# Squares queued behind splits, and a gates' and weight-sum workload spread over a recurrence, in a two-layer trunk kernel

## The chip, the cores and the metric

The kernel runs on one core of one Trainium2 chip. Five engines work at once, each through its own queue in order: TensorE (PE: matmuls), VectorE (DVE), ScalarE (ACT), GpSimd (POOL) and SyncE (SP, which here only issues transfers). ACT and POOL issue transfers too. The metric is the device time of one execution in microseconds; before the change the median of 3 runs is 1962.18 (1956.06 to 1965.04).

## What is computed

One sequence of 512 positions with 16 meta tokens ahead of it (T = 528), model width 2048, two residual layers and a final RMS norm, all in float32 at the interface:

```python
for layer in range(DEPTH):
    hn = rms_norm(h, norm_gain[layer])
    if layer % 2 == 0:
        y = even_mixer(...)   # GLU -> causal conv(31) -> LayerNorm -> swish, beside sparse attention; gates; @ w_out
    else:
        y = odd_mixer(...)    # 16 heads of a gated linear recurrence (HGRN2), RMS norm per head, gate; @ w_out
    h = h + y
h = rms_norm(h, final_norm_gain)
```

The sparse attention scores all keys with a small indexer, keeps the top 128 admissible ones of each query and attends to them with a shared relative bias. Most of the arithmetic lies in the dense projections: `hn @ w_in` and `@ w_out` of both layers.

## The kernel before

**Stripes.** A dense weight is cut into stripes of 128 output columns: 2048 x 128 float32, held as a [128, 2048] tile of 1 MB. A stripe goes through these steps: the load `w` (SP, L185, three buffers); a square with a running sum (ACT, L190, output `junk`); a sum over partitions, `tot` (POOL, L142); a power-of-two scale from it, `u`, `sc`, `inv` (DVE); the split of each half into a float16 high part `wh` (ACT, L206) and low part `wl` (DVE, L207), with five half buffers of each; then 96 matmuls into two banks of PSUM (48 into one bank for the stripes that need only 512 columns), three per block of 128 x 128: high by high, high by low, low by high (L245 to L247); and the evacuation (ACT or DVE). The names of weight tiles carry a number in the listings below: `w_476` and `w_669` are the first two split stripes of the even layer (the second is the first convolution stripe, g0), `w_791` and `w_947` the next two; `w_228` is an early stripe that is multiplied raw, without square and split. `w_8762` (before) and `w_8758` (after) are the first stripe of the even output projection.

**Stages.** The program loads x and its statistics, splits X0 (16 tiles `x`, L287 on ACT and L288 on DVE) and multiplies two stripes raw; then come the even layer's stripes with convolution (DVE, L576), indexer, softmax and attention between them; the even output projection of 16 stripes (S_OE), whose inputs MX are 16 split tiles, eight from the convolution branch (`x<-z`) and eight from the attention branch, which come back from DRAM (`mbd`) through the staging tile `mb`; the residual `h` (L764), also stored to `h1d`; the split X1; 16 heads of the recurrence, each with three stripes (fz, q, v) and some 70 small products (L833 to L972); 16 gates' stripes, whose scales are known by then (`gsc`); and the odd output projection, which works on pairs of stripes and on weight sums (`osum`, L1117).

**Early squares.** The scales of the gates' and the odd output projection's stripes come from squares taken ahead: `early_square` loads a whole stripe into a tile `gw` (one buffer, on ACT's queue, L745) and squares it. Those of the gates' stripes stand in the even output projection, one per stripe, the first gw load near the program's start; those of the odd output projection stand in the gates' stage, three per group for the first groups.

**Weight sums.** For seven pairs of odd output stripes, sums of half stripes are made in DRAM by transfers alone: 14 copies (SP, L324 and L325), 28 accumulating transfers (POOL, L327 and on) and 14 copies of one sum to the next (`os<-os`, SP, L330 and L334).

**What sets the order.** Each engine's queue is laid down when the program is built, by a planner that simulates it; of the work that could go next it takes that of the highest band: WGT (5), EVAC (4), SIDE (3), CONV (2). `tc.issue_after(ins)` puts what is issued under it behind that instruction in the same engine's queue; it adds no wait.

Of the kernel before, what the change touches and what calls it, by code (L numbers as in the profile page):

```python
# [74 lines left out]
def trunk_kernel(ctx: ExitStack, tc: tile.TileContext, x: bass.AP, w: bass.AP, wukv: bass.AP,  # L75
# [62 lines left out]

    EXP = float(2 ** 23)

    def all_sum(out, src, op=None):
        G.partition_all_reduce(out, src, channels=128, reduce_op=op or bass_isa.ReduceOp.add)  # L142
# [37 lines left out]
    def load_raw(s, pieces=1):  # L180

        w32 = wpool.tile([128, 2048], F32, name="w32", bufs=3)
        n = 2048 // pieces
        for i in range(pieces):
            Q.dma_start(w32[:, i * n:(i + 1) * n], w[s, :, i * n:(i + 1) * n])  # L185
# [16 lines left out]
    def split_weights(src, sc):  # L202

        hi = wpool.tile([128, 1024], F16, name="wh", bufs=5)
        lo = wpool.tile([128, 1024], F16, name="wl", bufs=5)
        S.activation(hi, src, AF.Identity, scale=sc)  # L206
        V.scalar_tensor_tensor(lo, src, sc, hi, op0=OP.mult, op1=OP.subtract)  # L207
        return hi, lo

    def load(s, back, keep=None, known=None):  # L210

        w32 = load_raw(s)
        if known is None:
            ss = wpool.tile([128, 1], F32, name="ss", bufs=4)
            square_sum(w32, ss)
            total = wpool.tile([128, 1], F32, name="tot", bufs=4) if keep is None else keep
            all_sum(total, ss)
            known = scales(total, back)
        sc, inv = known
        halves = [split_weights(w32[:, 1024 * n:1024 * (n + 1)], sc) for n in range(2)]  # L220
        return [h[0] for h in halves], [h[1] for h in halves], inv
# [98 lines left out]
    def sum_step(step, sa, sb, d):  # L320

        a1, a2, b1, b2 = w[sa, :, :1024], w[sa, :, 1024:], w[sb, :, :1024], w[sb, :, 1024:]
        if step == 0:
            Q.dma_start(d[0], b1)  # L324
            Q.dma_start(d[2], a1)  # L325
        elif step == 1:
            G.dma_start(d[0], b2, accum_op=OP.add)  # L327
            G.dma_start(d[2], b1, accum_op=OP.add)
        elif step == 2:
            Q.dma_start(d[1], d[0])  # L330
        elif step == 3:
            G.dma_start(d[1], a1, accum_op=OP.add)
        elif step == 4:
            Q.dma_start(d[3], d[1])  # L334
        elif step == 5:
            G.dma_start(d[3], a2, accum_op=OP.add)
# [369 lines left out]
    with band(SIDE):  # L706
        sums = cst([128, 8], F32, "mxb")
        for i in range(3):
            V.tensor_reduce(sums[:, i:i + 1], stat[:, i, :], axis=AX, op=OP.add)
        c = [sums[:, i:i + 1] for i in range(8)]  # L710
        sq = [vmax[:, i:i + 1] for i in range(6)]
        V.tensor_scalar(c[3], sq[2], 2048.0, None, op0=OP.mult)
        V.scalar_tensor_tensor(c[3], sq[3], 2.0, c[3], op0=OP.mult, op1=OP.add)
        V.tensor_tensor(c[3], c[3], c[0], op=OP.mult)
        V.scalar_tensor_tensor(c[4], c[2], 256.0, sq[4], op0=OP.mult, op1=OP.mult)
        V.tensor_tensor(c[4], c[4], c[1], op=OP.mult)
        V.tensor_tensor(c[3], c[3], c[4], op=OP.add)
# [20 lines left out]
    gss = r2p.tile([128, 16], F32, name="gss", bufs=1)  # L738
    gstat = r2p.tile([128, 16], F32, name="gstat", bufs=1)
    oss = r2p.tile([128, 16], F32, name="oss", bufs=1)  # L740

    def early_square(s, ss):
        with band(CONV):
            raw = wpool.tile([128, 2048], F32, name="gw", bufs=1)
            S.dma_start(raw, w[s])  # L745
            square_sum(raw, ss)
# [9 lines left out]
    for n in range(KT):  # L756
        with band(EVAC):
            while len(HIN) < min(KT, n + 3):
                residual0()
        hin = HIN[n]  # L760
        ps, inv = stripe(S_OE + n, MX, mback, order=(1, 0))
        with band(EVAC):
            for p, sl in ps:
                V.scalar_tensor_tensor(hin[:, sl], p, inv, hin[:, sl], op0=OP.mult, op1=OP.add)  # L764
# [12 lines left out]
    with band(EVAC):
        with tc.issue_after(last.ins):
# [62 lines left out]
    def rec_head(h, fz, q, v):  # L841
# [132 lines left out]
        V.tensor_tensor(on, o, rs, op=OP.mult)  # L974
        ON.append(on)

    for h in range(16):
        fz = ht([128, T], F32, "fz", 2)
        q = ht([128, SEQ], F32, "q", 2)
        v = ht([128, T], F32, "v", 2)  # L980
        if h == 0:
            with band(EVAC):
                evac(fz, ps0, rstd1)
        for dst, i in ((fz, 0), (q, 1), (v, 2)):
            if h or i:
# [25 lines left out]
        return t[:, :SEQ].bitcast(F16).rearrange("p (a b) -> p a b", a=2)  # L1011

    with band(SIDE):
        all_sum(gstat, gss)
# [12 lines left out]
        V.tensor_scalar(gs[:, 1:2], oscale, 0.5, None, op0=OP.mult)  # L1027

    def group(i):
# [3 lines left out]
        with band(SIDE):  # L1033
# [25 lines left out]
    with band(EVAC):  # L1059
        NP = KT // 2  # L1060
        opair = ht([128, NP], F32, "opair")
        V.tensor_reduce(opair, oss.rearrange("p (a b) -> p a b", b=2), axis=AX, op=OP.add)
        ototal = ht([128, NP], F32, "ototal")
        all_sum(ototal, opair)
        ou, osc, oinv = [ht([128, NP], I32, n) for n in ("ou", "osc", "oinv")]
        half_exponent(ou, ototal)
        V.tensor_scalar(osc, ou, -1.0, 204 * EXP, op0=OP.mult, op1=OP.add)
        V.tensor_scalar(oinv, ou, oback, None, op0=OP.add)
        osc, oinv = osc.bitcast(F32), oinv.bitcast(F32)
        oninv = ht([128, NP], F32, "oninv")  # L1070
        V.tensor_scalar(oninv, oinv, -1.0, None, op0=OP.mult)
# [227 lines left out]
```

## Time and profile before

| | us |
|---|---|
| median of 3 runs | 1962.18 |
| profiled execution | 1966.32 |
| its span | 1964.5 |
| PE busy | 1837.5 (94%) |
| DVE busy | 1340.1 (68%) |
| ACT busy | 1202.3 (61%) |
| POOL busy | 184.3 (9%) |

The profile is of one execution. A row of a timeline gives start, length, engine, line, operation, and in brackets the engine's idle time ahead of it with what ended it. A row of waits gives engine, name and line that waited, then what it waited for, with the total, the count and the longest. A wait is put down to the releaser that came last. The granted clock of PE is 1.00 at full speed and 0.50 at half.

### The profile page before, as it was taken

How to read it: one execution, taken by the hardware profiler on the slowest of the kernel's cores; microseconds unless marked ns; L12 is line 12 of the kernel's file. 1: busy time of each engine (PE TensorE's matmuls, PEld its weight loads, DVE VectorE, ACT ScalarE, POOL GpSimd, SP SyncE). 2: the span in 40 equal slices, each digit the busy share in tenths (PEclk: the TensorE clock that was granted, in tenths of full speed). 3: DMA queues.
4: the chain of work that ended last, by engine and by line, in shares of the span. 5: the costliest groups of instructions: out<-in, count | busy, mean ns of one | idle time of the engine just before them, and what ended most of it. 6: DMA issues, size and time to landing. Idle time of an engine off the chain costs nothing.

```text
span 1964.5 us, 36557 instructions
## 1 busy us (share of the span) xinstructions
PE 1837.5 (94%) x14934; PEld 1410.8 (72%) x14934; DVE 1340.1 (68%) x2752; ACT 1202.3 (61%) x1881; POOL 184.3 (9%) x324
## 2 busy tenths in 40 slices
PE   8499999888999989698989999999999999999997
PEld 6367668776888778487767777777777775445886
DVE  7249999997737335443468777787778776666775
ACT  5366566434555565675467776777677787545563
POOL 2122111001121210100010000000000000001000
PEclk9699999998999999799999999999999999999998
DMA  9997233222334324765422222222222266225653
GB/s 314 294 283 209 86 103 107 96 71 90 110 115 120 123 61 128 255 246 194 152 97 87 70 83 87 87 84 71 84 87 87 96 227 236 106 89 203 214 194 108
DMA packets 60825, 272.78 MB, mean 139 GB/s; under 512 B 7760, under 2 KB 15224, under 8 KB 39440
## 3 DMA queue, kind: packets, MB, share of 16 engines
q1 hardware_dynamic: 38592, 195.04, 27.6%
q0 software_dynamic: 15152, 37.51, 8.6%
q10 hardware_dynamic: 6912, 37.88, 5.3%
q8 instruction: 117, 1.92, 0.4%
q14 instruction: 52, 0.43, 0.1%
HBM read 251.30 MB, written 40.58 MB: 149 GB/s over the span
## 4 chain that ended last, share of the span: by engine, by line
PE 42%; issue 5%; DMA 5%; ACT 3%; DVE 1%; POOL 0%; ACTq 0%; DVEq 0%; POOLq 0%
PE mps L245 10%; PE mps L246 10%; PE mps L247 10%; PE mps L1117 8%; DMA gw<-in_w_dram 3%; DMA w<-in_w_dram 2%; ACT junk L190 2%; PE s L837 1%; PE s L838 1%; PE s L839 1%; PE po L960 1%; PE po L959 1%; PE s L956 0%; ACT wh L206 0%; DVE wl L207 0%
## 5 line engine op out<-in xcount | busy, mean ns | idle before, releaser
L245 PE MATMUL mps<-x,wh 128*128 128x264 f16 (+1 forms) x3440 | 1023.8, 298 | 70.6 <-ACT x L287 30.7
L246 PE MATMUL mps<-x,wh 128*128 128x264 f16 (+1 forms) x3440 | 1023.9, 298 | 4.2 <-DVE x L288 4.0
L247 PE MATMUL mps<-x,wl 128*128 128x264 f16 (+1 forms) x3440 | 1022.7, 298 | 0.4 <-DVE wl L207 0.4
L245 PEld LDWEIGHTS <-wh 128*128 128x128 f16 x3456 | 341.0, 99 | 167.1 <-issue 35.8
L246 PEld LDWEIGHTS <-wh 128*128 128x128 f16 x3456 | 341.1, 99 | 149.3 <-issue 37.4
L247 PEld LDWEIGHTS <-wl 128*128 128x128 f16 x3456 | 340.9, 99 | 121.2 <-issue 8.7
L207 DVE SCALAR_TENSOR_TENSOR wl<-w,sc,wh 128x1024 f16<-128x1024 f32 x224 | 287.1, 1285 | 141.3 <-ACT wh L206 133.1
L206 ACT ACTIVATE wh<-w,sc 128x1024 f16<-128x1024 f32 x224 | 254.4, 1144 | 152.8 <-PE mps L246 141.7
L190 ACT ACTIVATE junk<-w 128x2048 bf16<-128x2048 f32 (+1 forms) x116 | 216.2, 1864 | 144.6 <-DMA w<-in_w_dram 132.8
L576 DVE SCALAR_TENSOR_TENSOR z<-u,vec,z 128x528 f32<-128x528 f32 x240 | 179.3, 764 | 1.3
L142 POOL PARTITION_ALL_REDUCE tot<-ss x96 | 47.0, 489 | 885.9 <-ACT junk L190 885.9
L146 DVE TENSOR_SCALAR u<-tot 128x1 int32<-128x1 int32 x96 | 14.5, 151 | 152.0 <-POOL tot L142 151.8
L1117 PEld LDWEIGHTS <-wh 128*128 128x128 f16 x912 | 89.2, 98 | 11.0 <-issue 0.3
L206 ACT ACTIVATE wh<-w,osc 128x1024 f16<-128x1024 f32 x53 | 60.8, 1151 | 56.6 <-PE mps L1117 46.1
L207 DVE SCALAR_TENSOR_TENSOR wl<-w,osc,wh 128x1024 f16<-128x1024 f32 x53 | 67.8, 1283 | 30.5 <-ACT wh L206 30.4
L190 ACT ACTIVATE junk<-gw 128x2048 bf16<-128x2048 f32 x32 | 61.1, 1911 | 35.6 <-DMA gw<-in_w_dram 35.4
L1117 PE MATMUL mps<-on,wh 128*128 128x256 f16 x464 | 78.2, 273 | 0.1
L207 DVE SCALAR_TENSOR_TENSOR wl<-w,gsc,wh 128x1024 f16<-128x1024 f32 x32 | 41.1, 1283 | 37.4 <-ACT wh L206 37.2
L833 ACT ACTIVATE qhm<-q 128x256 f16<-128x256 f32 x128 | 51.7, 415 | 19.7 <-DVE q L935 14.6
L1117 PE MATMUL mps<-on,wl 128*128 128x256 f16 x232 | 63.2, 273 | 0.0
L834 DVE SCALAR_TENSOR_TENSOR qlm<-q,qhm 128x256 f16<-128x256 f32 x128 | 52.6, 421 | 11.1 <-ACT qhm L833 9.1
L206 ACT ACTIVATE wh<-w,gsc 128x1024 f16<-128x1024 f32 x32 | 36.6, 1145 | 23.3 <-PE mps L246 23.3
(430 smaller groups left out, 2756.1 us busy)
## 6 DMA issues: line engine op xcount, KB each, us to landing
w<-in_w_dram SPq DMA_DIRECT2D x132, 1024.0 KB, 4.9
gw<-in_w_dram ACTq DMA_DIRECT2D x32, 1024.0 KB, 4.9
os<-in_w_dram POOLq DMA_DIRECT2D x28, 512.0 KB, 18.3
w<-os SPq DMA_DIRECT2D x28, 512.0 KB, 4.2
w<-in_w_dram SPq DMA_DIRECT2D x23, 512.0 KB, 4.2
os<-in_w_dram SPq DMA_DIRECT2D x14, 512.0 KB, 21.4
os<-os SPq DMA_DIRECT2D x14, 512.0 KB, 12.3
h<-in_x_dram POOLq DMA_DIRECT2D x16, 264.0 KB, 5.2
```

Source lines behind the costliest of these rows:

```text
L142: G.partition_all_reduce(out, src, channels=128, reduce_op=op or bass_isa.ReduceOp.add)
L190: S.activation(junk[:, :src.shape[-1]], src, AF.Square, accum_out=ss)
L206: S.activation(hi, src, AF.Identity, scale=sc)
L207: V.scalar_tensor_tensor(lo, src, sc, hi, op0=OP.mult, op1=OP.subtract)
L245: P.matmul(o, hi[half][:, ws], xh[:, sl], start=n == 0 and k == 0, stop=False)
L246: P.matmul(o, hi[half][:, ws], xl[:, sl], start=False, stop=False)
L247: P.matmul(o, lo[half][:, ws], xh[:, sl], start=False, stop=n == 1 and k == 7)
L576: eng.scalar_tensor_tensor(z, u[:, j:j + T], col(V_CW + i * CW + j), z, op0=OP.mult, op1=OP.add)
L833: S.activation(hi, src, AF.Copy, scale=scale)
L834: V.scalar_tensor_tensor(lo, src, scale, hi, op0=OP.mult, op1=OP.subtract)
L837: P.matmul(out, kh, qh, start=True, stop=False)
L1117: P.matmul(p, wt[:, sl], xt, start=start and k == i == 0, stop=stop and k == 7 and i == 2, skip_group_check=stop and not start and resume)
```

## The change

Five things, by the diff:

1. In `load` a stripe's square is put, by `behind("S")`, behind the last split that was issued so far on ACT.
2. The gates' early squares leave the even output projection. They come in the recurrence: per head, two loads of half a stripe (two buffers) and, a head later, two squares of 1024 columns; `gsum` adds the halves.
3. The weight sums leave the start. `waves` lays out 56 transfers, `send` issues 1, 2 and 1 of them behind the `all_sum` of the three stripes of each head, all from POOL.
4. The eight attention tiles come back from DRAM through the staging names Kh, Vt and L (three buffers each), and seven of their splits go to new tiles `mx` of their own.
5. The odd output projection's early squares become halves too, one stripe per gates' stripe, behind a split, and their scales come in two blocks (`pair_scales`).

```diff
+    queued = {}
+
     def all_sum(out, src, op=None):
-        G.partition_all_reduce(out, src, channels=128, reduce_op=op or bass_isa.ReduceOp.add)
+        queued["G"] = G.partition_all_reduce(out, src, channels=128, reduce_op=op or bass_isa.ReduceOp.add)
...
-        S.activation(hi, src, AF.Identity, scale=sc)
+        queued["S"] = S.activation(hi, src, AF.Identity, scale=sc)
...
+    def behind(name):
+        return tc.issue_after(queued[name].ins) if name in queued else ExitStack()
...
-            square_sum(w32, ss)
+            with behind("S"):
+                square_sum(w32, ss)
...
+    def sum_steps(sa, sb, d):
 
         a1, a2, b1, b2 = w[sa, :, :1024], w[sa, :, 1024:], w[sb, :, :1024], w[sb, :, 1024:]
...
+        return [[(d[0], b1, 0), (d[2], a1, 0)], [(d[0], b2, 1), (d[2], b1, 1)], [(d[1], d[0], 0)],
+                [(d[1], a1, 1)], [(d[3], d[1], 0)], [(d[3], a2, 1)]]
+
+    def waves(first, sums):
+
+        steps = [sum_steps(first + 2 * p, first + 2 * p + 1, d) for p, d in enumerate(sums)]
+        return [t for h in range(len(sums) + 5) for p in range(len(sums)) if 0 <= h - p < 6 for t in steps[p][h - p]]
+
+    def send(todo, n):
+        with band(CONV), behind("G"):
+            for _ in range(min(n, len(todo))):
+                dst, src, add = todo.pop(0)
+                G.dma_start(dst, src, accum_op=OP.add if add else OP.bypass)
...
-            mb = et([128, T], F32, "mb", 2)
+            shape, name = (([128, T], "Kh"), ([128, 5, 128], "Vt"), ([128, T], "L"))[i // 3]
+            mb = et(shape, F32, name, 3)
...
-            MX[8 + i] = split(r1p.tile([128, 2, T], F16, name="x", bufs=KT), mb, c[7])
+            MX[8 + i] = split(r1p.tile([128, 2, T], F16, name="mx" if i < 7 else "x", bufs=7 if i < 7 else KT), mb, c[7])
...
+    def early_load(s):
+        for o in (0, 1024):
+            raw = ht([128, 1024], F32, "gw", 2)
+            S.dma_start(raw, w[s, :, o:o + 1024])
+            raws.append(raw)
...
-        early_square(S_G + n, gss[:, n:n + 1])
...
+    todo = waves(S_OO, osum)
...
+                send(todo, 1 + i % 2)
...
-            for p in range(7):
-                sum_step(h - p, S_OO + 2 * p, S_OO + 2 * p + 1, osum[p])
+            if h:
+                for c in range(2):
+                    square_sum(raws.pop(0), gss[:, h - 1, c:c + 1])
+            early_load(S_G + h)
...
+            with band(CONV), behind("S"):
+                if raws:
+                    for c in range(2):
+                        square_sum(raws.pop(0), oss[:, ahead - 1, c:c + 1])
+                if ahead < KT:
+                    early_load(S_OO + ahead)
+                ahead += 1
+            if ahead in (9, 17):
+                pair_scales(ahead // 16)
-        for n in range(3 * i, min(3 * i + 3, KT)):
-            early_square(S_OO + n, oss[:, n:n + 1])
         group(i)
```

What stands in the queues. On ACT, from the statistics to the first splits (L190 and L192 are the square, L206 and L208 the split of a weight, L287 and L293 that of X0), before and then after:

```order
L190 ACTIVATE junk,ss<-w_476 128x2048
L305 ACTIVATE rstd<-po,eps_r 128x264
L305 ACTIVATE rstd<-s_288,eps_r 128x264
L306 ACTIVATE rstd<-rstd 128x264 x2
L206 ACTIVATE wh<-w_476,sc 128x1024 x2
L287 ACTIVATE x<-sq,gains 128x528 x13
L190 ACTIVATE junk,ss<-w_669 128x2048
L287 ACTIVATE x<-sq,gains 128x528 x3
L437 ACTIVATE sq<-gb 128x528
L206 ACTIVATE wh<-w_669,sc 128x1024 x2
```

```order
L192 ACTIVATE junk,ss<-w_669 128x2048
L293 ACTIVATE x<-sq,gains 128x528 x3
L208 ACTIVATE wh<-w_669,sc 128x1024 x2
L192 ACTIVATE junk,ss<-w_791 128x2048
L293 ACTIVATE x<-sq,gains 128x528
L420 ACTIVATE kih<-gt 128x528
L293 ACTIVATE x<-sq,gains 128x528 x2
L208 ACTIVATE wh<-w_791,sc 128x1024
L293 ACTIVATE x<-sq,gains 128x528 x4
L459 ACTIVATE z<-s_607 8x352
L293 ACTIVATE x<-sq,gains 128x528 x2
L208 ACTIVATE wh<-w_791,sc 128x1024
```

The square of `w_669` now stands ahead of all X0 splits and its split behind three of them, and the square of `w_791` ahead of the other thirteen. In SP's queue the load of `w_669` stands right behind that of `w_476`; before, the 14 copies of the weight sums stood between them.

On ACT, at the end of the even layer's stripes and the first stripes of the output projection (`gw` are gates' stripes, `x<-z` the splits of the convolution branch), before and then after:

```order
L287 ACTIVATE x<-z,mxb 128x528 x8
L190 ACTIVATE junk,gss<-gw 128x2048
L767 ACTIVATE acc_8621<-h_8625 128x528
L772 DMA h1d<-h_8625 128x528
L190 ACTIVATE junk,ss<-w_8762 128x2048
L745 DMA gw<-in_w_dram 128x2048
L190 ACTIVATE junk,gss<-gw 128x2048
L190 ACTIVATE junk,ss<-w_8893 128x2048
L745 DMA gw<-in_w_dram 128x2048
L206 ACTIVATE wh<-w_8762,sc 128x1024 x2
L206 ACTIVATE wh<-w_8893,sc 128x1024 x2
```

```order
L208 ACTIVATE wh<-w_8758,sc 128x1024
L274 ACTIVATE gt<-mps,inv 128x264
L591 ACTIVATE gb<-gt 128x528
L293 ACTIVATE x<-L,mxb 128x528
L293 ACTIVATE x<-z,mxb 128x528 x6
L208 ACTIVATE wh<-w_8758,sc 128x1024
L192 ACTIVATE junk,ss<-w_8885 128x2048
L293 ACTIVATE x<-z,mxb 128x528
L274 ACTIVATE gt<-mps,inv 128x264
L703 ACTIVATE gt<-z 128x528
L274 ACTIVATE gt<-mps,inv 128x264
L591 ACTIVATE gb<-gt 128x528
```

The split of the first output stripe now stands among the MX splits, with no gates' square ahead of it; before, three squares and two loads stood between the last MX split and it.

On POOL, in the first heads of the recurrence, after the change (`tot` is the sum of a stripe's squares, `os` a weight sum in DRAM):

```order
L144 ISA tot<-ss 128x1
L341 DMA os_156<-os_155 16x8192
L878 MEMSET vt 128x128
L144 ISA tot<-ss 128x1
L341 DMA os_159<-in_w_dram 128x1024
L144 ISA tot<-ss 128x1
L341 DMA os_161<-in_w_dram 128x1024
L341 DMA os_163<-in_w_dram 128x1024
L144 ISA tot<-ss 128x1
L341 DMA os_165<-in_w_dram 128x1024
```

Before, this queue held in this stage only `tot` and the clearing of `vt`; each transfer now stands behind one stripe's `tot` and ahead of the next one's.

More of the change, by code (lines that the diff above doesn't have):

```diff
@@ L184, in load_raw @@
         for i in range(pieces):
-            Q.dma_start(w32[:, i * n:(i + 1) * n], w[s, :, i * n:(i + 1) * n])
+            queued["Q"] = Q.dma_start(w32[:, i * n:(i + 1) * n], w[s, :, i * n:(i + 1) * n])
         return w32
@@ L318, in trunk_kernel @@
     osum = [[dram.tile([128, 1024], F32, name=f"os{p}{i}") for i in range(4)] for p in range(7)]
-    def sum_step(step, sa, sb, d):
+    def sum_steps(sa, sb, d):
         a1, a2, b1, b2 = w[sa, :, :1024], w[sa, :, 1024:], w[sb, :, :1024], w[sb, :, 1024:]
[L323 to L336, printed above, removed]
+        return [[(d[0], b1, 0), (d[2], a1, 0)], [(d[0], b2, 1), (d[2], b1, 1)], [(d[1], d[0], 0)],
[8 more added lines that the diff above has]
+                G.dma_start(dst, src, accum_op=OP.add if add else OP.bypass)
     r1 = tc.tile_pool(name="r1", bufs=KT, side="left")
@@ L722, in trunk_kernel @@
         for i in range(8):
-            mb = et([128, T], F32, "mb", 2)
+            shape, name = (([128, T], "Kh"), ([128, 5, 128], "Vt"), ([128, T], "L"))[i // 3]
+            mb = et(shape, F32, name, 3)
+            if len(shape) > 2:
+                mb = mb.rearrange("p a b -> p (a b)")[:, :T]
             Q.dma_start(mb, mbd[i])
-            MX[8 + i] = split(r1p.tile([128, 2, T], F16, name="x", bufs=KT), mb, c[7])
+            MX[8 + i] = split(r1p.tile([128, 2, T], F16, name="mx" if i < 7 else "x", bufs=7 if i < 7 else KT), mb, c[7])
         for i in range(8):
@@ L737, in trunk_kernel @@
     back1 = xscale[1][1]
-    gss = r2p.tile([128, 16], F32, name="gss", bufs=1)
+    gss = r2p.tile([128, 16, 2], F32, name="gss", bufs=1)
     gstat = r2p.tile([128, 16], F32, name="gstat", bufs=1)
[L740 to L746, printed above, removed]
+    oss = r2p.tile([128, 16, 2], F32, name="oss", bufs=1)
+    raws = []
+    def early_load(s):
[3 more added lines that the diff above has]
+            raws.append(raw)
     H1 = []
@@ L766, in trunk_kernel @@
             if n == 0:
-                S.activation(acc1, hin, AF.Square)
+                done = S.activation(acc1, hin, AF.Square)
             else:
                 sq = U.tile([128, T], F32, name="sq1", bufs=3)
-                last = S.activation(sq, hin, AF.Square)
+                done = S.activation(sq, hin, AF.Square)
                 V.tensor_tensor(acc1, acc1, sq, op=OP.add)
             S.dma_start(h1d[n], hin)
-        early_square(S_G + n, gss[:, n:n + 1])
     with band(WGT):
@@ L777, in trunk_kernel @@
     with band(EVAC):
-        with tc.issue_after(last.ins):
+        with tc.issue_after(done.ins):
             S.preload_act_table_set("natural_log_exp_and_others")
@@ L1013, in trunk_kernel @@
     with band(SIDE):
-        all_sum(gstat, gss)
+        for c in range(2):
+            square_sum(raws.pop(0), gss[:, 15, c:c + 1])
+        gsum = ht([128, 16], F32, "gsum")
+        V.tensor_reduce(gsum, gss, axis=AX, op=OP.add)
+        all_sum(gstat, gsum)
         gu = ht([128, 16], I32, "gu")
@@ L1041, in group, with pair_scales @@
             FB[i] = split(form_slot(SLOTS[2 * i + 1]), xb, gs[:, 1:2])
+    oq = ht([128, 5, 8], F32, "oq")
+    osc, oinv, oninv = oq[:, 2, :].bitcast(I32), oq[:, 3, :].bitcast(I32), oq[:, 4, :]
+    def pair_scales(c):
+        sl = slice(4 * c, 4 * c + 4)
+        with band(EVAC):
+            V.tensor_reduce(oq[:, 0, sl], oss[:, 8 * c:8 * c + 8, :].rearrange("p (a b) c -> p a (b c)", b=2),
+                            axis=AX, op=OP.add)
+            all_sum(oq[:, 1, sl], oq[:, 0, sl])
+            u = ht([128, 4], I32, "ou", 2)
+            half_exponent(u, oq[:, 1, sl])
+            V.tensor_scalar(osc[:, sl], u, -1.0, 204 * EXP, op0=OP.mult, op1=OP.add)
+            V.tensor_scalar(oinv[:, sl], u, oback, None, op0=OP.add)
+            V.tensor_scalar(oninv[:, sl], oinv[:, sl].bitcast(F32), -1.0, None, op0=OP.mult)
+    ahead = 1
+    early_load(S_OO)
     for i in range(8):
@@ L1054, in trunk_kernel @@
                 V.scalar_tensor_tensor(ON[h], ON[h], col(V_RG + h), g[:, :SEQ], op0=OP.mult, op1=OP.mult)
-        for n in range(3 * i, min(3 * i + 3, KT)):
-            early_square(S_OO + n, oss[:, n:n + 1])
-        group(i)
[L1059 to L1071, printed above, removed]
+            with band(CONV), behind("S"):
+                if raws:
+                    for c in range(2):
+                        square_sum(raws.pop(0), oss[:, ahead - 1, c:c + 1])
[4 more added lines that the diff above has]
+                pair_scales(ahead // 16)
+        group(i)
+    osc, oinv = osc.bitcast(F32), oinv.bitcast(F32)
     acc2 = ht([128, SEQ], F32, "sg", 2)
```

## The prediction

> **What bounds the kernel now.** I read the table of stretches first, then what TensorE (PE) waits for, then the timelines around each wait. TensorE is busy almost all of the span, so only stretches in which it is not, or runs at a lower granted clock, have time to give.
>
> Stretches (start:end, length, then busy time and instructions of PE, weight load, DVE, ACT, POOL, then granted clock, DMA share, GB/s):
>
> ```profile
> 40.00:80.00 40.00, 14.21 (x103) 12.03 (x102) 12.76 (x21) 6.24 (x8) 8.70 (x13) 0.71 1.03 271
> 80.00:120.00 40.00, 38.41 (x255) 26.21 (x255) 14.15 (x27) 23.13 (x31) 7.23 (x13) 0.87 1.00 293
> 200.00:360.00 160.00, 159.81 (x1152) 117.19 (x1151) 155.31 (x334) 95.64 (x164) 19.48 (x28) 1.00 0.32 105
> 360.00:490.00 130.00, 109.77 (x878) 90.86 (x877) 113.58 (x242) 52.90 (x86) 14.63 (x25) 0.95 0.26 80
> 780.00:830.00 50.00, 31.87 (x246) 25.19 (x245) 23.14 (x38) 31.28 (x38) 9.13 (x18) 0.80 0.65 232
> 1030.00:1600.00 570.00, 569.00 (x5433) 442.48 (x5431) 441.00 (x1042) 422.18 (x712) 19.38 (x58) 1.00 0.25 91
> 1600.00:1640.00 40.00, 37.84 (x298) 24.59 (x297) 27.34 (x60) 32.28 (x53) 0.00 (x0) 1.00 0.61 225
> ```
>
> PE loses 26 of 40 us at 40–80, 20 of 130 at 360–490, 18 of 50 at 780–830, and 1 of 570 in the recurrence, which is PE-bound. The waits of PE (us in total, times, longest) name who comes last:
>
> ```profile
> PE mps L245 <- ACT x L287: 30.7, 7, 27.2
> PE mps L245 <- ACT wh L206: 15.3, 1, 15.3
> ...
> PE mps L245 <- DVE h L764: 9.8, 6, 2.7
> ...
> PE s L538 <- DMA uh<-ql: 5.4, 2, 3.8
> ```
>
> Most of it is ACT. In the list for all engines, ACT itself waits mostly in front of squares (L190), for their loads:
>
> ```profile
> ACT junk L190 <- DMA w<-in_w_dram: 132.8, 46, 28.5
> ACT junk L190 <- DMA gw<-in_w_dram: 35.4, 22, 5.8
> ```
>
> A queue runs in order, so a square that waits for its load holds up the splits and evacuations behind it. That is what the parts of the change touch.
>
> **1. The start (T1).** ACT's timeline; the bracket is idle time before the row and its releaser:
>
> ```profile
> 32.42 1.98 ACT L287 ACTIVATE x<-sq,gains 128x528 f16<-128x528 f32 x3
> 37.68 1.99 ACT L287 ACTIVATE x<-sq,gains 128x528 f16<-128x528 f32 x3 [3.29 <-DVE sq L383]
> ...
> 49.49 0.74 ACT L287 ACTIVATE x<-sq,gains 128x528 f16<-128x528 f32 x1 [1.24 <-DVE sq L383]
> 78.70 1.91 ACT L190 ACTIVATE junk<-w 128x2048 bf16<-128x2048 f32 x1 [28.48 <-DMA w<-in_w_dram]
> ...
> 99.82 0.48 ACT L563 ACTIVATE gt<-mps,inv 128x264 f32<-128x264 f32 x1 [2.22 <-PE mps L247]
> ```
>
> Thirteen of the sixteen X0 splits are done at 50.2; the other three stand behind the square of w_669, whose load lands only at 78.7. The last evacuation of that stripe, g0, is at 99.82. SP's queue and the page's list of DMA issues (KB, median us to landing) say why the load is late:
>
> ```profile
> 43.90 7.97 SPq L185 DMA_DIRECT2D w<-in_w_dram  x3
> ```
> ```profile
> w<-in_w_dram SPq DMA_DIRECT2D x132, 1024.0 KB, 4.9
> ...
> os<-in_w_dram SPq DMA_DIRECT2D x14, 512.0 KB, 21.4
> ```
>
> w_669 is issued at 43.90, behind the 14 os copies, into DMA engines that are full (share 1.03) with them, the POOL accumulates and a gw load. In the change nothing of this is ahead of w_669, which goes out right behind w_476 and should be there when its square comes up near 30. Next late: the square of w_791. It stands behind the first three X0 splits and the split of w_669, ahead of the other thirteen, and its buffer is that of the raw stripe w_228, still being multiplied. SP got all three buffers by 43.9 + 8.0 = 51.9, so that load lands between 43.9 + 4.9 = 48.8 and 56.8. I take 49: square done at 51. Then thirteen splits at the pace shown (ten from 37.68 to 50.23, 1.25 each) are 16.3, the two splits of w_791 2.2, and I allow 3.5 for evacuations between: the last X0 at 73. The order leaves about 69 matmuls of g0 behind it. One matmul, in the out-projection where they run close:
>
> ```profile
> 888.75 0.27 PE L245 MATMUL mps<-x,wh 128*128 128x264 f16 x1 [1.71 <-DVE h L764]
> 888.87 0.27 PE L246 MATMUL mps<-x,wh 128*128 128x264 f16 x1
> ```
>
> 0.113 from start to start, so 7.8: g0 ends near 81 against 99.8. **T1 = −18**; with the load at 56.8 and something over for a slow clock it is −8, with no blocking at all −27, the whole wait.
>
> **2. The attention's first scores (T2).**
>
> ```profile
> 147.24 0.39 PE L538 MATMUL s<-kih,uh 128*128 128x256 f32 x1 [3.83 <-DMA uh<-ql]
> ```
>
> The 5.4 of waits there (list above) are a small transfer behind the same full DMA engines. In the stretch that follows, and in one of part 4, the granted clock is 0.50 (the columns as in the first table):
>
> ```profile
> 804.10:821.20 17.10, 3.64 (x17) 2.23 (x18) 5.73 (x10) 11.12 (x13) 0.76 (x2) 0.50 0.55 198
> 148.70:155.50 6.80, 6.10 (x26) 4.66 (x27) 5.68 (x10) 3.23 (x6) 0.00 (x0) 0.50 1.04 266
> ```
>
> PE is busy 6.1 of 6.8 us at half speed, so up to 3 more is lost. The transfers are gone from there; I take 5.4 and half of that 3: **T2 = −7** (0, if the copy itself is slow, to −8).
>
> A clock of one half after a long wait is also a rule of the Trainium skill ("TensorE: Matmul & The Clock Gate", Part 1): the clock halves after an idle window of about 3.4 us and comes back after a busy one. The trace agrees: its half-clock stretches above last 6.8 and 17.1 us, two and five such windows. By the rule alone each removed long wait would also give half of one such window; the sum uses the stretches of the trace.
>
> **3. Even stripes at 374–482 (T3).** The waits of PE in that stretch alone:
>
> ```profile
> PE mps L245 <- ACT gt L268: 7.3, 6, 2.6
> ...
> PE mps L245 <- ACT gt L563: 5.6, 5, 1.5
> ```
>
> These 12.9 are on a bank of PSUM whose evacuation, by the order, stands behind another item in ACT's queue. The new order puts one square between two splits at a fixed place, and fewer stripes start both banks on the one just before. But DVE is busy 113.6 of 130 there, so the stretch may not shrink much: **T3 = −6** (0 to −13), half of the waits.
>
> **4. Into the even out-projection (T4).** ACT again, then PE:
>
> ```profile
> 798.58 1.90 ACT L190 ACTIVATE junk<-gw 128x2048 bf16<-128x2048 f32 x1
> ...
> 810.91 1.91 ACT L190 ACTIVATE junk<-gw 128x2048 bf16<-128x2048 f32 x1 [5.79 <-DMA gw<-in_w_dram]
> ...
> 814.91 4.26 ACT L206 ACTIVATE wh<-w,sc 128x1024 f16<-128x1024 f32 x4
> ```
> ```profile
> 817.14 0.40 PE L245 MATMUL mps<-x,wh 128*128 128x264 f16 x1 [15.30 <-ACT wh L206]
> ```
>
> The splits of the first two out-projection stripes stand behind two squares of gates' stripes (gw) and a 5.79 wait for one; PE stands 15.3. In the change no gw is there, and w_8758's square and split stand among the MX splits. What goes: 15.3, some 2 of the smaller X waits ahead of it (the rest of the 30.7 above beside 27.2 is 3.5), and half of the 3.6 that PE ran at half clock (row 804.10). **T4 = −19** (−8, if the mx splits from DRAM hold ACT up, to −21.6).
>
> **5. Out-projection stripes (T5).** The chain of waits repeats itself each 12.7 us (start, length, what):
>
> ```profile
> 901.07 6.18 DMA w<-in_w_dram
> ...
> 909.37 2.01 ACT junk L190 x2
> 911.37 1.05 ACT wh L206
> 912.44 1.29 DVE wl L207
> 913.75 6.12 DMA w<-in_w_dram
> ```
>
> One load, two squares (one for the stripe, one for the gates), split, and the next load into the buffer that this frees: 6.2 + 2.0 + 2.0 + 1.1 + 1.3 = 12.6. A split waits for the square of a later stripe, and that one for a load that needs the split's buffer. With the square behind the split the loop is broken; PE's own 96 × 0.113 = 10.8 is left. Five or six stripes: 9.8 of waits and one lower-clock window. **T5 = −11** (−5 to −11.3).
>
> **6. The recurrence (T6, T7).** Its last head and the gates' start lose 2.2 of 40 (row 1600); gw squares then go behind no load: **T6 = −2** (0 to −2). Added to each of 16 heads: two squares of 1024 (2 × 1.0), two DMA issues, four transfers from POOL. The nearest rows for ACT that full and for POOL's issues:
>
> ```profile
> 1560.00:1612.00 52.00, 51.37 (x455) 36.58 (x453) 33.54 (x73) 43.62 (x68) 0.59 (x2) 1.00 0.56 204
> ```
> ```profile
> 27.95 0.93 POOL L327 DMA_DIRECT2D os<-in_w_dram  x1 [21.15 <-DMA os<-in_w_dram]
> ```
>
> With ACT at 84% and DMA at 0.56 PE loses 0.63 in 52; over 590 us that is 7. The added work gives ACT 74 + 6 = 80%. **T7 = +6** (0 to +32, two a head, as in the last one).
>
> The moved MX staging, gsum, the halved odd squares and pair_scales lie beside PE-bound stretches (160–360, 1640–1945) and cost nothing while ACT has a quarter free; without that cover some 2 us.
>
> Sum: −18 − 7 − 6 − 19 − 11 − 2 + 6 = −57. The profiled execution is 1966.3, 4.1 above the median of the runs, so 1909 there, **1905** as a median.
>
> **Rivals.**
> A. The even stage is bound by DVE (155 of 160 us busy at 200–360, 113.6 of 130 after). Then an earlier start only makes DVE's backlog wait later: T1 to T3 (31) come back, 1936. Against it: DVE had 27 of 80 us at 40–120, so its queue starts early too.
> B. Slower: POOL's queue in the recurrence. An accumulate follows its copy by one stripe (10.8 us) at the head and tail of the waves. If the copy has not landed, POOL stands, and the sum `tot` of a later stripe stands behind it, then its split, then PE. The slack is a stripe less the square and that sum (a group of the page, mean ns behind the comma), 10.8 − 2.0 − 0.5, about 8.
>
> ```profile
> L142 POOL PARTITION_ALL_REDUCE tot<-ss x96 | 47.0, 489 | 885.9 <-ACT junk L190 885.9
> ```
>  Waits of 21.2 have been seen (row 27.95), with the DMA full; 13 over the slack in 14 heads is +180, and from 4 a head the whole gain is gone; at 7 a head, 2005. For it: POOL now issues plain copies too. Against: DMA share of 0.25 there.
>
> The Trainium skill ("DMA: Bandwidth & Descriptors", SWDGE vs HWDGE vs iDMA) speaks for B: descriptors of GpSimd's transfers are written to SBUF, where DVE can lock it out, while those of SP are immune, so that 28 copies would lose by the move. No row of before shows a plain copy from POOL in a busy stage.
>
> C. The out-projection keeps its pace: evacuations on DVE (h L764) or the MX staging hold it and T4, T5 come to a third: 1925.
>
> **Numbers.** Forecast 0.60, A 0.15, C 0.14, B 0.06; 0.05 that the pieces cancel to about no change. The range 1884 to 1942 holds the first three cases; below 1884 T1, T3 and T4 would all have to reach their far ends. Faster by over 0.5% (what a measurement of this kernel can tell) 0.88, within 0.05, slower 0.07.
>
> **What shows it.** PE's wait at 81 under 10 us and no ACT wait of 28; PE's 15.3 gone near 800; a period of 10.8 from h to h; no uh wait; PE still over 99% in the recurrence and no POOL `os` wait over 8. Wrong if `tot` waits for os, or if g0 still ends after 95.

## The result, and the profile after

The changed kernel takes 1873.39 us (median of 4 runs, 1871.17 to 1874.84), the one before 1960.51 (1956.06 to 1965.04): a ratio of 0.9555, with a 95% interval of 0.9529 to 0.958. That is 87 us less where 57 were forecast, and below the range's lower end of 1884. The direction was right, the size was not.

The profiled execution after takes 1873.82 with a span of 1872.0, against 1966.32 and 1964.5: 92.5 less. That execution of the kernel before was 5.8 over its median, and the one after 0.4, so a few us of what follows are the spread of single executions. PE's busy time fell from 1837.5 to 1815.4, its idle time from 127.0 to 56.6. So 70 us of the gain are waits, and 22 are PE's own time, for the same number of matmuls (14934) at a mean granted clock of 0.986 where it was 0.972.

To place the gain I took from both traces the start of the n-th high-by-high matmul of the stripes (3456 of them, the same work in nearly the same order) and subtracted. The prediction's terms against it, in us:

| stretch (by matmul number) | forecast | profiled |
|---|---|---|
| start, 0 to 288 | T1 + T2 = −25 | −36.4 |
| middle of the even stripes, 288 to 960 | T3 = −6 | −24.4 |
| rest of the even stripes, 960 to 1440 | 0 | +3.9 |
| into the out-projection, 1440 to 1536 | T4 = −19 | −16.9 |
| out-projection stripes, 1536 to 1920 | T5 = −11 | −12.4 |
| X1, 1920 to 2016 | 0 | −2.0 |
| recurrence, 2016 to 3168 | T7 = +6 | −1.3 |
| gates, 3168 to 3456 | T6 = −2 | −2.8 |
| sum | −57 | −92.3 |

The table of stretches of the changed kernel, columns as before:

```profile
40.00:80.00 40.00, 40.00 (x292) 32.09 (x291) 28.33 (x49) 26.56 (x42) 5.72 (x13) 1.00 0.51 132
80.00:120.00 40.00, 40.00 (x309) 30.33 (x308) 34.98 (x58) 22.15 (x32) 2.77 (x6) 1.00 0.27 88
605.00:637.00 32.00, 11.96 (x95) 10.01 (x93) 5.57 (x7) 8.34 (x11) 10.36 (x8) 0.71 0.14 48
1030.00:1450.00 420.00, 420.00 (x4011) 325.16 (x4009) 325.74 (x775) 332.84 (x560) 40.55 (x83) 1.00 0.52 161
```

PE is busy 40 of 40 where it had 14 and 38, at full clock. The recurrence stays at 100% though ACT and POOL do more and the DMA share is twice as high. One stretch is worse: at 605 to 637 PE stands for 20 of 32 us. The waits of PE after:

```profile
PE s L304 <- POOL acc L681: 20.0, 1, 20.0
PE s L628 <- ACT L L619: 5.8, 4, 2.8
PE s L409 <- DVE qh L279: 5.2, 1, 5.2
PE mps L251 <- ACT gt L274: 5.1, 3, 3.8
PE mps L251 <- ACT x L293: 2.2, 1, 2.2
...
PE mps L251 <- ACT gt L568: 1.9, 3, 0.7
```

The waits on X0, on wh, on h and on uh are gone (the 2.2 on x is on X1, at 932.64), those on gt fell from 14.9 to 7.0. Two waits are longer. At the start PE waits 5.2 for `qh`, where it waited 2.8 at the same place for `sc`. And the wait on `acc`, the sum of squares of the convolution branch's layer norm, is 20.0; before it was this row:

```profile
PE s L298 <- POOL acc L676: 6.0, 1, 6.0
```

The start, on ACT, after:

```profile
30.80 1.90 ACT L192 ACTIVATE junk<-w 128x2048 bf16<-128x2048 f32 x1
...
32.69 1.98 ACT L293 ACTIVATE x<-sq,gains 128x528 f16<-128x528 f32 x3
34.78 2.19 ACT L208 ACTIVATE wh<-w,sc 128x1024 f16<-128x1024 f32 x2
36.87 1.89 ACT L192 ACTIVATE junk<-w 128x2048 bf16<-128x2048 f32 x1
...
78.25 0.46 ACT L568 ACTIVATE gt<-mps,inv 128x264 f32<-128x264 f32 x1
```

The square of w_669 runs at 30.80 without a wait, that of w_791 at 36.87, and g0's last evacuation is at 78.25 against 99.82. POOL before the long wait:

```profile
598.90 0.60 POOL L144 PARTITION_ALL_REDUCE stat<-ss  x1
609.49 9.07 POOL L681 TENSOR_TENSOR acc<-acc,sq 128x528 f32<-128x528 f32 x6 [9.99 <-issue]
626.13 0.40 POOL L144 PARTITION_ALL_REDUCE stat<-ss  x1 [7.57 <-issue]
633.71 1.28 POOL L681 TENSOR_TENSOR acc<-acc,sq 128x528 f32<-128x528 f32 x1 [7.18 <-issue]
```

Six of the seven additions, a partition sum of a later stripe, and the seventh addition, with gaps of 7.2 to 10.0 for which the profile shows no releaser. Before, the seven stood in one piece:

```profile
673.18 0.58 POOL L142 PARTITION_ALL_REDUCE stat<-ss  x1 [3.39 <-ACT junk L190]
680.48 10.44 POOL L676 TENSOR_TENSOR acc<-acc,sq 128x528 f32<-128x528 f32 x7 [6.72 <-issue]
```

### The profile page after: what moved, and what is told of

Its sections match the earlier page's. It is cut to its first block, busy times and chain, and to the rows that moved or that the text cites. A ratio compares the mean times of both kernels' runs of the same rounds, so it can differ in the third digit from the quotient of the medians.

```text
span 1872.0 us, 36780 instructions
## 1 busy us (share of the span) xinstructions
PE 1815.4 (97%) x14934; PEld 1405.2 (75%) x14934; DVE 1339.1 (72%) x2758; ACT 1203.5 (64%) x1941; POOL 194.7 (10%) x353
## 4 chain that ended last, share of the span: by engine, by line
PE 89%; DVE 4%; DMA 3%; ACT 2%; issue 2%; POOL 1%; SPq 0%; DVEq 0%; POOLq 0%; ACTq 0%
PE mps L252 23%; PE mps L251 23%; PE mps L253 23%; PE mps L1145 8%; PE po L635 1%; PE s L610 1%; DVE mask L556 1%; PE s L267 1%; DVE m L555 1%; PE s L846 1%; PE s L845 1%; PE s L847 1%; PE po L968 1%; PE po L967 1%; DMA w<-in_w_dram 1%
## 5 line engine op out<-in xcount | busy, mean ns | idle before, releaser
L251 PE MATMUL mps<-x,wh 128*128 128x264 f16 (+1 forms) x3216 | 955.8, 297 | 5.4 <-ACT x L293 2.2
L252 PE MATMUL mps<-x,wh 128*128 128x264 f16 (+1 forms) x3216 | 956.0, 297 | 1.7 <-DVE x L294 1.7
L253 PE MATMUL mps<-x,wl 128*128 128x264 f16 (+1 forms) x3216 | 955.7, 297 | 0.0
L208 ACT ACTIVATE wh<-w,sc 128x1024 f16<-128x1024 f32 x224 | 256.0, 1145 | 260.3 <-PE mps L252 225.1
L209 DVE SCALAR_TENSOR_TENSOR wl<-w,sc,wh 128x1024 f16<-128x1024 f32 x224 | 287.4, 1284 | 141.3 <-ACT wh L208 140.8
L192 ACT ACTIVATE junk<-w 128x2048 bf16<-128x2048 f32 (+1 forms) x116 | 214.7, 1851 | 3.7 <-DMA w<-in_w_dram 3.1
L1145 PEld LDWEIGHTS <-wh 128*128 128x128 f16 x912 | 89.2, 98 | 10.9 <-issue 0.3
L208 ACT ACTIVATE wh<-w,oq 128x1024 f16<-128x1024 f32 x53 | 60.7, 1148 | 54.6 <-PE mps L1145 46.3
L209 DVE SCALAR_TENSOR_TENSOR wl<-w,oq,wh 128x1024 f16<-128x1024 f32 x53 | 67.8, 1283 | 27.9 <-ACT wh L208 27.7
L192 ACT ACTIVATE junk<-gw 128x1024 bf16<-128x1024 f32 x64 | 67.3, 1052 | 2.1 <-DMA gw<-in_w_dram 0.8
L251 PE MATMUL mps<-mx,wh 128*128 128x264 f16 x224 | 62.3, 278 | 3.8 <-ACT gt L274 3.8
L842 DVE SCALAR_TENSOR_TENSOR qlm<-q,qhm 128x256 f16<-128x256 f32 x128 | 52.5, 420 | 17.0 <-ACT qhm L841 16.9
L841 ACT ACTIVATE qhm<-q 128x256 f16<-128x256 f32 x128 | 51.4, 415 | 18.4 <-DVE q L943 18.3
L253 PE MATMUL mps<-mx,wl 128*128 128x264 f16 x224 | 62.4, 279 | 0.0
L252 PE MATMUL mps<-mx,wh 128*128 128x264 f16 x224 | 62.4, 279 | 0.0
```

The source lines that it names most:

```text
L192: S.activation(junk[:, :src.shape[-1]], src, AF.Square, accum_out=ss)
L208: queued["S"] = S.activation(hi, src, AF.Identity, scale=sc)
L251: P.matmul(o, hi[half][:, ws], xh[:, sl], start=n == 0 and k == 0, stop=False)
L252: P.matmul(o, hi[half][:, ws], xl[:, sl], start=False, stop=False)
L253: P.matmul(o, lo[half][:, ws], xh[:, sl], start=False, stop=n == 1 and k == 7)
L841: S.activation(hi, src, AF.Copy, scale=scale)
```

## The experiments

All are timed against the kernel before on the same chip, whose medians were 1961.91, 1961.21 and 1960.93 in the three batches. Deltas by stretch, from the traces as above (one profiled execution of each kernel, from 2.4 under its median to 6.3 over it):

| run | start | 288–960 | 960–1440 | T4 | T5 | X1 | recurrence | gates | median |
|---|---|---|---|---|---|---|---|---|---|
| the change | −36.4 | −24.4 | +3.9 | −16.9 | −12.4 | −2.0 | −1.3 | −2.8 | 1873.39 |
| e1 change, additions on DVE | −35.5 | −24.5 | −15.5 | −17.5 | −12.4 | −2.0 | −1.2 | −2.8 | 1853.77 |
| e2 before, additions on DVE | −2.6 | −1.0 | −7.2 | +1.8 | −1.2 | +0.1 | +0.1 | +0.3 | 1951.63 |
| e3 change without part 1 | −33.7 | −5.2 | −4.2 | −21.1 | −12.4 | +0.8 | +56.5 | −2.7 | 1939.69 |
| e4 before with part 1 | −2.5 | −18.3 | +3.3 | −1.3 | −12.4 | −1.9 | −1.4 | +1.8 | 1933.19 |
| e5 change without part 3 | −7.0 | +1.1 | +2.8 | −17.1 | −12.4 | −2.0 | −1.2 | −2.8 | 1921.21 |
| e6 before with part 3 | −34.9 | −11.3 | −11.5 | −0.2 | −1.1 | +7.9 | +5.8 | +0.9 | 1921.77 |
| e7 change without part 2 | −36.6 | −24.6 | +4.0 | −6.8 | −10.7 | −1.9 | −1.4 | −2.8 | 1886.19 |
| e8 change without part 4 | −37.2 | −22.9 | +4.1 | −18.8 | −12.4 | −2.0 | −1.3 | −2.8 | 1872.51 |
| e9 change without 1 and 2 | −34.6 | −8.6 | −3.9 | −9.6 | +24.0 | +8.2 | +4.1 | −5.0 | 1938.34 |
| e10 change without 1 and 3 | −8.9 | +5.0 | +13.4 | −20.4 | −12.5 | −1.7 | +32.2 | −2.7 | 1966.10 |
| e11 e1 without part 4 | −38.0 | −24.6 | −16.6 | −19.1 | −12.4 | −2.0 | −1.3 | −2.8 | 1851.94 |

**The layer norm's wait (e1, e2).** One line, in the changed kernel and in the one before:

```diff
-                    G.tensor_tensor(vs_, vs_, sq, op=OP.add)
+                    V.tensor_tensor(vs_, vs_, sq, op=OP.add)
```

> The changed kernel, with the seven additions of the layer norm's squares (L681) on DVE in place of POOL. Theory R: POOL pays about 7 us each time it goes from the partition sum to the tensor addition or back (its unexplained gaps of 10.0, 7.3 and 7.2 us at 599 to 633); the change cut the seven additions in two and so put two more such turns before the one matmul that waits 20.0 us. Without turns the wait falls to under 4 us and the time to 1850 to 1858 (15 to 23 less than 1873.4). Rival Q: the gaps are POOL waiting for squares that stand late in ACT's queue; then DVE waits there too and the time stays within 6 of 1873.

> The kernel before with the same edit alone. Theory R: its one pair of turns stood before a wait of 6.0 us and some half clock; 4 to 9 less, 1951 to 1957. Rival Q: no difference beyond 2 us.

Measured: 1853.77 (ratio 0.9445, 0.9411 to 0.9479) and 1951.63 (0.9946, 0.9929 to 0.9963), both in theory R's bounds. The stretch 605 to 637 of e1:

```profile
605.00:637.00 32.00, 32.00 (x279) 28.41 (x277) 19.44 (x34) 27.24 (x51) 0.77 (x2) 1.00 0.25 84
```

PE is busy all of it, at full clock. The trace has two instructions of POOL's sequencer at each turn between the two kinds of work, which a timeline does not print: one pair of turns before, two pairs after. The additions' line in the changed kernel, and the chain of work around the later turns (POOLq is POOL's sequencer):

```profile
L681 POOLq MODIFY_POOL_CONFIG  x4: 83/83/83, 599.4 to 626.5; - x4
```
```profile
618.79 0.00 POOLq L144
618.80 7.33 issue
626.13 0.40 POOL stat L144
626.53 0.07 POOLq L681 x2
626.60 7.11 issue
633.71 1.29 POOL acc L681
```

These two turns take 7.2 and 7.6 us between the work on either side, where the inputs had long been there (the last square in front of the sum ended at 617.2, the sum began at 626.13). In all traces that keep the additions on POOL, no such turn, either way, is under 5.5 us from that instruction to the next work. By the Trainium skill ("GPSIMD Engine Reference", 2.1 Instruction dispatch), the first call to freshly loaded code on GpSimd pays about 6 us with no visible instruction; the trace's 7.2 is near that. That the time goes into loading code was not measured.

The wait goes with the order of the queue: with the seven in one piece it is 4.1 (e3, e6, e9), 6.0 (before), 10.9 (e4) and 11.6 (e5), and cut in two by a partition sum 18.0 (e10) and 20.0 to 20.2 (the change, e7, e8). The edit of e1 does two things, though: it takes the turns away, and an addition lasts 0.7 on DVE where it took 1.3 on POOL, some 4 us over seven. Its 19.6 are for both.

**Part 1, the squares' place (e3, e4).** The edit, undone in the changed kernel and made alone in the one before:

```diff
-            with behind("S"):
-                square_sum(w32, ss)
+            square_sum(w32, ss)
```

> The changed kernel with part 1 undone: the planner places a stripe's square where it likes. Theory S (the gain of 27 us in the middle of the even stage comes from the squares' place): it comes back between the 576th and the 960th high-by-high matmul, 15 to 27 us, and the out-projection's stripes lose 5 to 10 more; 1893 to 1910. Rival D (that gain is the convolution's backlog on DVE, which starts 36 us earlier because the weight sums are gone from the start): the middle stays, and only the out-projection may lose up to 10; 1870 to 1884. The start is as in the changed kernel by both, since the sums stay away.

> The kernel before with part 1 alone. Theory S: 15 to 27 less in the middle and 5 to 10 less in the out-projection, nothing at the start; 1925 to 1942. Rival D: nothing in the middle, 5 to 10 in the out-projection; 1948 to 1957.

Measured: 1939.69 (0.9865, 0.9816 to 0.9914) for e3, 1933.19 (0.9846, 0.9811 to 0.9882) for e4. e4 is as theory S had it, with 2.4 more in the out-projection's stripes; in e3 these lost nothing, against S. In e3 the middle does lose 19 of its 24 us, but both theories missed what is three times as much: the recurrence is 56.5 longer. ACT's waits there (1050 to 1500), SP's, and two squares in ACT's timeline with what stands behind the second, and PE's wait for it over the whole run, all of e3:

```profile
ACT junk L192 <- DMA w<-in_w_dram: 77.3, 30, 5.0
```
```profile
SPq L187 <- DVE wl L209: 184.8, 11, 17.9
```
```profile
1264.59 1.91 ACT L192 ACTIVATE junk<-w 128x2048 bf16<-128x2048 f32 x1 [4.99 <-DMA w<-in_w_dram]
...
1297.84 1.91 ACT L192 ACTIVATE junk<-w 128x2048 bf16<-128x2048 f32 x1 [3.46 <-DMA w<-in_w_dram]
...
1299.75 0.61 ACT L840 ACTIVATE kt0h<-k 128x512 f16<-128x512 f32 x1
1300.27 0.58 ACT L952 ACTIVATE kk<-s 128x512 f32<-128x512 f32 x1
```
```profile
PE s L960 <- ACT kk L952: 28.7, 13, 4.1
```

A square waits for its load, the load waits on SP for a buffer that a split (wl, L209) frees, and the copies that PE's next products need (kk) stand behind the square: this is the loop of the prediction's term T5, now in the recurrence's heads. In the same stage the squares' waits for `w` are 1.9 us in total before, and none in the changed kernel.

**Part 3, the weight sums (e5, e6).** e5 puts them back into the changed kernel, e6 moves them alone in the kernel before:

```diff
-    todo = waves(S_OO, osum)
...
-                send(todo, 1 + i % 2)
...
+            for p in range(7):
+                sum_step(h - p, S_OO + 2 * p, S_OO + 2 * p + 1, osum[p])
```

> The changed kernel with part 3 undone: the weight sums' copies and accumulates are back where the kernel before had them, ahead of the second stripe's load at the start. My theory: the start's 36 us come back (wait of 27 for the X0 splits, the uh wait, half clock), the middle keeps its gain (the squares' place gave 18 of it in the kernel before), the recurrence is as it is, since its transfers cost it nothing; the layer norm's additions stand in one piece again, some 10 less: 1895 to 1912. Rival D (the middle's gain came half from the earlier start): 10 to 14 more, 1908 to 1925.

> The kernel before with part 3 alone. My theory: 36 less from the start, nothing else lost: 1918 to 1930. Rival D: up to 14 more gained in the middle: 1908 to 1918. Rival B of the prediction: the transfers make POOL's sums late in the recurrence without part 1, where the run with the squares free lost 56: 1950 to 1985.

Measured: 1921.21 (0.9808, 0.9786 to 0.9831) and 1921.77 (0.9803, 0.9786 to 0.982). The start belongs to part 3: −34.9 with it alone, −7.0 without it. e5 is longer than my theory had it and within rival D's figure, since its middle gains nothing; e6's total lies where my theory put it and outside D's, but not by my theory, which had nothing but the start: 22.8 more were gained from 288 to 1440, as D would have it in the middle, and 13.7 lost at X1 and in the recurrence. That the total still fits is luck. Rival B is refuted for transfers alone: the recurrence of e6 is 5.8 longer, not 56, and with part 1 it is as before. The middle (the matmuls 576 to 960) of the kernel before, the changed one, e4, e6 and e5, in that order:

```profile
355.30:545.90 190.60, 167.30 (x1367) 140.63 (x1366) 157.30 (x330) 86.67 (x155) 23.60 (x40) 0.96 0.29 89
```
```profile
321.20:485.10 163.90, 158.00 (x1361) 136.33 (x1359) 148.21 (x305) 87.99 (x156) 26.25 (x43) 1.00 0.36 109
```
```profile
352.10:525.00 172.90, 162.62 (x1366) 137.99 (x1365) 154.59 (x324) 86.73 (x155) 27.78 (x40) 0.99 0.33 98
```
```profile
328.10:499.70 171.60, 164.24 (x1396) 140.48 (x1395) 147.39 (x304) 89.56 (x169) 28.06 (x47) 1.00 0.35 103
```
```profile
348.30:540.00 191.70, 165.81 (x1367) 140.45 (x1365) 159.88 (x341) 87.66 (x157) 26.61 (x43) 0.93 0.30 88
```

And what PE waited for in it, before and then after:

```profile
PE mps L245 <- ACT gt L268: 8.5, 7, 2.6
PE s L623 <- ACT L L614: 7.3, 4, 3.9
PE mps L245 <- ACT gt L563: 5.6, 5, 1.5
```
```profile
PE s L628 <- ACT L L619: 2.8, 1, 2.8
PE mps L251 <- ACT gt L568: 1.9, 3, 0.7
PE mps L251 <- ACT gt L274: 1.3, 2, 0.7
```

In this piece, 26.7 shorter in all, the bank waits fall by 10.9 (14.1 to 3.2), the waits of the softmax and its products by 6.5, and PE's busy time by 9.3. Most of the 9.3 can be the clock: granted 0.96 on average and then 1.00, which over 190.6 us is worth up to 7.6. Each part alone takes 18 to 19 off the piece (190.6 to 172.9 and to 171.6), both 27; part 3 alone gives 7.7 of it back just before, between the matmuls 288 and 576, which is why the table has only −11.3 for e6. So neither theory S nor D holds alone. e5, which has part 1 without part 3 as e4 has, does not keep the gain of e4: there one softmax wait grew:

```profile
PE s L629 <- ACT L L620: 19.9, 2, 16.3
```

Why that one wait came up in e5 was not tried.

**Parts 2 and 4, the gates' squares and the staging (e7, e8).** e7 takes the gates' squares from the recurrence and puts them, as two halves with two buffers, back into the out-projection; e8 restores the staging of the attention tiles:

```diff
+                raw = U.tile([128, 1024], F32, name="gw", bufs=2)
+                S.dma_start(raw, w[s, :, 1024 * c:1024 * c + 1024])
+                square_sum(raw, gss[:, n, c:c + 1])
```

```diff
-            shape, name = (([128, T], "Kh"), ([128, 5, 128], "Vt"), ([128, T], "L"))[i // 3]
-            mb = et(shape, F32, name, 3)
+            mb = et([128, T], F32, "mb", 2)
...
-            MX[8 + i] = split(r1p.tile([128, 2, T], F16, name="mx" if i < 7 else "x", bufs=7 if i < 7 else KT), mb, c[7])
+            MX[8 + i] = split(r1p.tile([128, 2, T], F16, name="x", bufs=KT), mb, c[7])
```

> The changed kernel with part 2 undone: the gates' squares are back in the even output projection, as two halves with two buffers, and gone from the recurrence. My theory: the step into the out-projection is slow again (a wait of some 10 to 15 for the first splits, with half clock), its later stripes stay at 10.8, the recurrence is unchanged: 1885 to 1896. Rival: the wait came from the attention tiles' staging (part 4), which is still the new one here: 1870 to 1877.

> The changed kernel with part 4 undone: attention tiles through two buffers mb and no mx tiles of their own. My theory: the splits of the first output stripes stand early by part 2 alone, so 0 to 4 more: 1872 to 1878. Rival (the staging gave half of that step): 8 to 12 more, 1881 to 1886.

Measured: 1886.19 (0.9628, 0.9607 to 0.9649) and 1872.51 (0.9552, 0.9535 to 0.9569); both as my theory had them. T4 is part 2 in the main: with the gates' squares back 10 of its 17 us are lost, and the wait for the first splits is there again (e7):

```profile
PE mps L251 <- ACT wh L208: 10.8, 1, 10.8
```

Every run with part 2 has 17 to 21 there, those with the squares back as halves (e7, e9) 7 to 10, those with them back whole (e4, e6) 0 to 1. What the halves keep was not taken apart further. Part 4 is worth nothing that these runs can tell.

T5 comes from either part. e4 has part 1 alone and still a gates' square in each stripe, and its ACT timeline has no wait for a load, at a period of 10.8:

```profile
871.95 1.90 ACT L192 ACTIVATE junk<-w 128x2048 bf16<-128x2048 f32 x1
...
873.97 1.91 ACT L192 ACTIVATE junk<-gw 128x2048 bf16<-128x2048 f32 x1
...
876.44 1.15 ACT L208 ACTIVATE wh<-w,sc 128x1024 f16<-128x1024 f32 x1 [0.47 <-PE mps L253]
...
882.75 1.90 ACT L192 ACTIVATE junk<-w 128x2048 bf16<-128x2048 f32 x1
```

Its splits wait for PE now, not PE for them. e3 has part 2 alone there and gains the same 12.4.

**What slows the recurrence when the squares are free (e9, e10).** Both have part 1 undone; e9 part 2 as well (as in e7), e10 part 3 as well (as in e5).

> Parts 1 and 2 undone: squares placed freely, the gates' squares back in the out-projection; the transfers still in the recurrence. With the squares free and everything else of the change (run before) the recurrence lost 56 us. Theory G (the gates' squares fill ACT's queue, so that a stripe's square, placed early, waits for a load whose buffer an item behind it frees): without them the recurrence is back to within 5 of the kernel before, but the out-projection is as slow as before; 1905 to 1925. Theory P (POOL's transfers hold up the partition sums): the 56 stay, 1950 to 1975.

> Parts 1 and 3 undone: squares placed freely, the weight sums back at the start; the gates' squares in the recurrence. Theory G: the recurrence loses 35 to 60 again, the start is as slow as before, the middle gains at most 10, the out-projection is fast: 1955 to 1990. Theory P: no loss in the recurrence, 1905 to 1930.

Measured: 1938.34 (0.9889, 0.986 to 0.9918) and 1966.10 (1.0029, 1.0014 to 1.0045). The recurrence is 4.1 longer than before in e9 and 32.2 longer in e10, so it is the gates' squares that make free squares dear there: theory G, somewhat under its figure in e10. The transfers alone add 4 to 6 (e9, and 5.8 in e6), and 24 where the gates' squares stand there too (e10 against e3). e9's total missed my figure, because its out-projection lost 24.0 (forecast as slow as before). Two half squares with two loads per stripe in a free order seem to be worse than one whole one (e6: −1.1), but e9 differs from e6 in parts 4 and 5 as well, and this was not tried apart.

**The best of it (e11).** e1 with part 4 undone.

> The changed kernel without part 4 and with the layer norm's additions on DVE. Both edits were run apart (0.9 less and 19.6 less); they touch different places, so 1852 to 1855. If the mx tiles only cost nothing because the layer norm's wait stood ahead of them, it is 4 to 10 more, 1857 to 1863.

Measured: 1851.94 (0.9452, 0.9424 to 0.9481), 0.06 under the first figure and against the second; the fastest kernel here, though its interval overlaps that of e1. Against the changed kernel it is 21 less.

## Why the prediction was wrong in size

The sizes of T1, T2 and T3 were too small, T3's cause was half of what it should have been, T7's cost did not come, and one wait stood in no term. The far ends of all terms together give −83, so the range's 1884 was near the most that the terms could give; what went past it is T3, with some of T2.

**T1 and T2: mis-sized, 25 for 36.4.** The cause was right (e6: the weight sums alone). By the starts of the high-by-high matmuls, the 40th and the 168th are both 25 earlier and the 184th, behind the attention's first scores, 36: so T1 is 25 where 18 were forecast, and T2 11 where 7 were. The failed step of T1 is "that load lands between 48.8 and 56.8. I take 49": I took SP's issue of three loads in the kernel before as a bound for w_791. In the changed kernel that load went out at 31.4 and landed at 36.3, with the DMA share at 0.47 (30 to 40) where it had been 1.01; its square ran at 36.87 with no wait, and the last X0 split ended at 61.9, not 73. Nothing of the 27.2 stayed, but the first matmuls start 4.5 to 6 later than before, after the wait for `qh`. The first 288 matmuls of both kernels:

```profile
0.00:207.90 207.90, 168.84 (x1090) 122.18 (x1091) 126.34 (x241) 111.10 (x154) 47.01 (x76) 0.90 0.91 265
```
```profile
0.00:171.60 171.60, 164.47 (x1091) 120.33 (x1092) 141.76 (x262) 100.89 (x146) 21.17 (x48) 0.98 0.44 145
```

Idle time falls from 39.1 to 7.1, and PE's busy time by 4.4 more with the granted clock up from 0.90 to 0.98; T2 priced only 1.5 of such loss. What else T2's 11 hold beside its wait of 5.4 and this was not followed up.

**T3: mis-sized, 6 for 24.4; its range ended at 13.** Three steps failed. The term took the squares' place for the whole cause, where part 3 alone shortens the piece from 576 to 960 as much (e6). The term counted only the bank waits, not those of the softmax (6.5 less), and nothing of PE's own time (9.3 less in 576 to 960, most of it by the clock). And "DVE is busy 113.6 of 130 there, so the stretch may not shrink much" was wrong: DVE's work in the piece fell with it only from 157.3 to 148.2, and 148 of 164 is 90%, where it had been 83%. A high busy share was room taken, not a bound.

**The layer norm: missing.** A wait of 6.0 in the kernel before stood in no term; it became 20.0. What the change put between the additions was one partition sum. e1 and e2 price it. It counts against the change: 19.6 less in e1 and 10.3 less in e2 leave 9 that the change added. Without them the forecast would have been off by 9 more, so part of its error was hidden by luck.

**T4 and T5: right**, 19 for 16.9 and 11 for 12.4, the latter 1.1 past its far end; that the square's place makes the loop I described for T5 is what e4 shows, with the addition that removing the gates' square breaks it as well (e3). T6, 2 for 2.8, right in kind, 0.8 past its end.

**T7: +6 for −1.3.** The nearest row I took (84% ACT, 0.63 lost in 52 us) was of a place where squares waited for their loads. The added work costs nothing with part 1 and 32 to 56 without it, more than the 32 at the range's end.

**Rivals.** A did not come: the middle gained. C did not come. B did not come in the changed kernel. A loss of its price, and at its place, came in e3 (56.5), but by ACT's queue and not by POOL's: e9 has the same transfers in the same queue and loses 4.1. (B's own sum at 7 a head in 14 heads is 98, so 2003 and not 2005.) The rule of the Trainium skill cited for it ("DMA: Bandwidth & Descriptors", SWDGE vs HWDGE vs iDMA) shows no cost here: 56 transfers from POOL cost the changed kernel's recurrence nothing, with DVE busy 325.74 of 420. No run here shows whether DVE ever locked POOL out.

**A reading that was off.** I wrote that ACT itself waits mostly in front of squares. Its longest row before is another one, a split that waits for PE; the squares' two rows make 168.2:

```profile
ACT wh L206 <- PE mps L246: 175.2, 86, 4.9
```

The expected signs came: no 27 at the start, no 15 at the out-projection, a period of 10.8, PE over 99% in the recurrence.

## What to carry to other kernels

A pre-pass (here a square for a scale) that waits for its load should be queued behind the work of the item ahead that frees load buffers; placed earlier, it makes a loop through the buffers, which here cost 12.4 in the out-projection's stripes and 56 in the recurrence, where other work shares the queue. When a wait is removed, price the lower clock that follows it too: PE's own busy time gave 22 of the 92 us. And look at what an engine's queue order newly interleaves: one foreign instruction between two of POOL's additions made a wait of 11 to 12 (e4, e5) one of 20.

## What the runs showed of the hardware that was not expected

- A turn of POOL between a partition sum and a tensor addition takes 7.2 to 7.6 us in the changed kernel, in which the profile shows no work and no releaser, only MODIFY_POOL_CONFIG at its head; additions on DVE, without turns, are worth 10 us in the kernel before (e2) and 20 in the changed one, which has two pairs of turns (e1).
- Stripes of 96 matmuls keep a period of 10.8 with a gates' square of 2 us in each on ACT (e4), so ACT had room for it all along; only the place of the squares in its queue was wrong.
